# A hybrid encoder trunk: the first eight steps in a written order with x in eighths, and two pieces of background work put off by a step

## The chip, the cores and the metric

The kernel runs on one core of a Trainium2 chip. The metric is the device time in microseconds (us) of one execution, the median over runs. The engines are named as the profile names them: PE is TensorE (matmuls and transposes), PEld its weight loads, DVE is VectorE, ACT is ScalarE, POOL is GpSimd, SP is SyncE, which issues nearly all loads.

## The reference

Two layers over 256 tokens of width 2048, in float32. Each layer normalises x, projects it to queries, keys and values of three groups of heads, runs three kinds of attention (A: a window of 128 tokens with a sink and a learned bias; B: a neighbourhood on a grid with a learned bias; C: global, with normalised and rotated queries and keys), normalises each group's output, projects it back, and adds an MLP with a squared ReLU. Cut to what matters:

```python
for l in range(DEPTH):                      # DEPTH = 2
    h = rmsnorm(x, norm_mix[l])
    proj = h @ w_in[l]                      # 2048 -> 3840
    qa, ka, va, qb, kb, vb, qc, kc, vc = split(proj)
    oa = window_attention(qa, ka, va, a_sink[l], t5_table)        # 8 heads
    ob = neighborhood_attention(qb, kb, vb, b_rpb[l])             # 8 heads
    oc = axial_global_attention(qc, kc, vc, c_q_gain[l], c_k_gain[l])   # 16 heads
    mix = concat([rmsnorm(oa, out_gain_a[l]), rmsnorm(ob, out_gain_b[l]), rmsnorm(oc, out_gain_c[l])])
    x = x + mix @ w_o[l]
    h = rmsnorm(x, norm_mlp[l])
    u = relu(h @ w_up[l])                   # 2048 -> 8192
    x = x + (u * u) @ w_down[l]
return rmsnorm(x, norm_final)
```

## The kernel before

All of x (two tiles of 128 tokens) stays in the on-chip memory; the weights are streamed through once, in pieces of 512 KB. Every float32 product is made of three products of shorter numbers: a weight piece is split into a high part (ACT, line 823) and a low part (DVE, line 824), an activation likewise, and high x high, high x low and low x high are added up in PSUM.

One weight piece is one **step**. The list `steps` is walked in order (lines 852 to 871). Per layer, counted from 0: steps 0 to 59 are the input projection (queries of A, keys and values of A, keys and values of C, queries of C twice, values of B, and two chunks b0 and b1 with queries and keys of B); steps 60 to 67 the output projection of group A, 68 to 83 that of C, 84 to 91 that of B; then come the steps of the MLP. A step of the projections is 12 matmuls of 512 columns in `mode_b` (steps 8 to 11 have 24 of 256 columns), for each of the two token tiles in the order high-high, high-low, low-high per weight row block. A step's weights are loaded seven steps ahead and split two steps ahead.

Everything else (transposes, softmax, products with V, preparing a mixer block) is **background work**: `add` (line 150) puts a piece with a cost and a delay into the queue `bgq`, and `tick` (line 163), called after each step, moves a clock on by 2.6 and emits pieces that are due, from the front of the queue, until the next piece would exceed a budget of 2.2. `need(flag)` (line 176) is called before a step whose input must be there: while the flag is not set, it emits the piece at the front of the queue, whether due or not. A program-level scheduler then orders each engine's instructions near that order; on the chip each engine runs its own instructions strictly in order and waits on semaphores for the others.

One attention **unit** (four score blocks: four heads of one kind, or two heads for two query blocks in B) is three pieces: scores and softmax (`unit_scores`, lines 333 to 372: scores into the one score bank `S`, bias on DVE, row maximum, exponentials on ACT, reciprocal, normalising on POOL at line 372), transposes of the probabilities (`unit_transp`, line 381, split by ACT and DVE at 382 and 383), and the product with V (`unit_pv`, lines 393 and 400, summed by DVE at 408 and 413). Each layer has four units of B; they are called U1 to U4. After the last unit of a block of heads, `unit_pv` calls `u.finish`, which is `mix_prep` (line 417): it makes the high and low parts of the block (lines 423 and 424) and sums squares on POOL; with a group's last block it also sets the flag ("mix", layer, group), which the group's first output step needs.

The queries' transposes (`q_transposes`, lines 254 to 261) and the keys' (`k_transposes`, lines 269 to 276) of b0 and b1 are two pieces with the same delay after the projection's end. Transposes, products with V and the steps' results share six PSUM banks; a bank is free when DVE has read its last user.

The start: `hprep` transposes x, scales it by the norm's gain and splits it (lines 199 to 211), and sums squares of x (line 190) whose reciprocal root (line 244) is applied when a projection's result leaves PSUM (line 539). x is loaded in two pieces of 256 columns and three of 512, with weight pieces between them on SP's queue. A matmul with a bias table (line 136) is one more background piece.

## Time and profile before

| | us |
|---|---|
| median of 3 runs | 2062.93 (2062.06 to 2064.14) |
| the profiled execution | 2063.2 |
| its span in the profile | 2061.4 |
| PE busy | 2042.8 |
| DVE busy | 1337.5 |
| ACT busy | 1049.7 |
| POOL busy | 256.6 |

The span runs from the first to the last recorded instruction; 1.8 us of the execution's own time lie outside it. A busy time is the sum of an engine's instructions; PE's are pipelined, so two neighbours overlap in the record and the distance between their starts is what one costs. In rows of the timeline the first number is the start, the second the length, and the bracket at the end says how long the engine stood idle before and what ended that.

### The profile page before, as it was taken

How to read it: one execution, taken by the hardware profiler on the slowest of the kernel's cores; microseconds unless marked ns; L12 is line 12 of the kernel's file. 1: busy time of each engine (PE TensorE's matmuls, PEld its weight loads, DVE VectorE, ACT ScalarE, POOL GpSimd, SP SyncE). 2: the span in 40 equal slices, each digit the busy share in tenths (PEclk: the TensorE clock that was granted, in tenths of full speed). 3: DMA queues.
4: the chain of work that ended last, by engine and by line, in shares of the span. 5: the costliest groups of instructions: out<-in, count | busy, mean ns of one | idle time of the engine just before them, and what ended most of it. 6: DMA issues, size and time to landing. Idle time of an engine off the chain costs nothing.

```text
span 2061.4 us, 27426 instructions
## 1 busy us (share of the span) xinstructions
PE 2042.8 (99%) x10424; PEld 1739.4 (84%) x10424; DVE 1337.5 (65%) x1629; ACT 1049.7 (51%) x1544; POOL 256.6 (12%) x294
## 2 busy tenths in 40 slices
PE   8999999999999999999999999999999999999998
PEld 7888788888888888888888888888888888888887
DVE  6777976565565555656668789766565556556565
ACT  6667756444344444444556676555344444434444
POOL 0393330000000000000005744200000000000001
PEclk9999999999999999999999999999999999999999
DMA  8655465666666666666656463566666666666663
GB/s 285 179 169 157 155 192 179 190 186 192 195 186 194 192 194 192 187 194 186 188 178 183 152 181 113 184 184 185 195 188 194 189 194 192 186 195 186 193 212 123
DMA packets 107681, 381.26 MB, mean 185 GB/s; under 512 B 11891, under 2 KB 14707, under 8 KB 107548
## 3 DMA queue, kind: packets, MB, share of 16 engines
q1 hardware_dynamic: 107116, 378.41, 60.4%
q8 instruction: 82, 1.34, 0.3%
q10 hardware_dynamic: 432, 1.10, 0.1%
q14 instruction: 51, 0.42, 0.1%
HBM read 377.34 MB, written 2.11 MB: 184 GB/s over the span
## 4 chain that ended last, share of the span: by engine, by line
PE 96%; DVE 1%; ACT 1%; issue 1%; DMA 0%; SPq 0%; DVEq 0%; POOLq 0%; POOL 0%; ACTq 0%
PE mm L465 19%; PE mm L466 19%; PE mm L467 19%; PE mm L630 17%; PE mm L634 9%; PE S L630 6%; PE S L634 3%; PE tr L381 1%; PE tr L400 1%; PE S L339 1%; PE S L340 1%; PE tr L199 1%; DMA wraw<-in_w_in_dram 0%; DVE big L424 0%; PE tr L393 0%
## 5 line engine op out<-in xcount | busy, mean ns | idle before, releaser
L824 DVE TENSOR_TENSOR wlo<-wraw,whi 128x1024 fp32r<-128x1024 f32 (+1 forms) x697 | 861.0, 1237 | 648.5 <-ACT whi L823 640.4
L823 ACT CAST whi<-wraw 128x1024 fp32r<-128x1024 f32 (+1 forms) x697 | 730.5, 1050 | 913.9 <-PE mm L467 460.6
L465 PE MATMUL mm<-whi,big 128*128 128x512 f32 (+1 forms) x1800 | 696.7, 388 | 6.8 <-DVE big L261 3.7
L466 PE MATMUL mm<-wlo,big 128*128 128x512 f32 (+1 forms) x1800 | 694.8, 386 | 1.0 <-DVE wlo L824 0.9
L467 PE MATMUL mm<-whi,big 128*128 128x512 f32 (+1 forms) x1800 | 693.5, 385 | 0.0
L630 PE MATMUL mm<-big,whi 128*128 128x512 f32 x1536 | 417.0, 393 | 0.0
L465 PEld LDWEIGHTS mm<-whi,big 128*128 128x128 f32 x1800 | 338.9, 188 | 72.3 <-issue 4.1
L467 PEld LDWEIGHTS mm<-whi,big 128*128 128x128 f32 x1800 | 339.1, 188 | 67.7
L466 PEld LDWEIGHTS mm<-wlo,big 128*128 128x128 f32 x1800 | 339.4, 189 | 66.2 <-DVE wlo L824 2.1
L630 PEld LDWEIGHTS mm<-big,whi 128*128 128x128 f32 x1536 | 272.9, 189 | 44.5
L634 PE MATMUL mm<-big,wlo 128*128 128x256 f32 x1536 | 245.0, 282 | 0.0
L634 PEld LDWEIGHTS mm<-big,wlo 128*128 128x128 f32 x1536 | 227.7, 190 | 20.0
L630 PE MATMUL S<-big,whi 128*128 128x512 f32 x512 | 158.6, 390 | 0.0
L372 POOL TENSOR_SCALAR big<-big,sm 128x256 f32<-128x256 f32 x128 | 87.2, 699 | 244.3 <-DVE sm L370 156.0
L630 PEld LDWEIGHTS S<-big,whi 128*128 128x128 f32 x512 | 96.2, 188 | 22.0
L244 POOL TENSOR_TENSOR sm<-sm,mhalf 128x2 f32<-128x2 f32 (+2 forms) x12 | 12.3, 1029 | 780.9 <-DVE sm L239 767.4
L634 PE MATMUL S<-big,wlo 128*128 128x256 f32 x512 | 103.2, 283 | 0.0
L718 POOL TENSOR_TENSOR x<-x,big 128x512 f32<-128x512 f32 x6 | 8.6, 1454 | 718.1 <-ACT mid L725 718.1
L670 DVE SCALAR_TENSOR_TENSOR x<-mm,sm,x 128x512 f32<-128x512 f32 x127 | 89.2, 743 | 3.1 <-PE mm L467 3.1
L634 PEld LDWEIGHTS S<-big,wlo 128*128 128x128 f32 x512 | 79.4, 191 | 0.0
L361 ACT ACTIVATE big<-S,sm,rq 128x256 f32<-128x256 f32 x64 | 35.3, 561 | 19.9 <-DVE sm L347 17.2
L645 DVE SCALAR_TENSOR_TENSOR mid<-mid 128x512 f32<-128x512 f32 x64 | 43.9, 686 | 0.5
(127 smaller groups left out, 1185.6 us busy)
## 6 DMA issues: line engine op xcount, KB each, us to landing
wraw<-in_w_up_dram SPq DMA_DIRECT2D x256, 512.0 KB, 3.5
wraw<-in_w_down_dram SPq DMA_DIRECT2D x256, 512.0 KB, 3.5
wraw<-in_w_in_dram SPq DMA_DIRECT2D x119, 512.0 KB, 3.6
wraw<-in_w_o_dram SPq DMA_DIRECT2D x64, 512.0 KB, 4.3
biasB<-in_rpb_dram SPq DMA_DIRECT2D x16, 349.5 KB, 6.3
biasA<-avec SPq DMA_DIRECT2D x4, 768.0 KB, 4.8
x<-in_x_dram SPq DMA_DIRECT2D x3, 512.0 KB, 8.6
big<-in_gfin_dram SPq DMA_DIRECT2D x2, 512.0 KB, 5.6
```

Of the source, the lines that this page charges most:

```text
L199: last_tr[0] = nc.tensor.transpose(psv[:, kk, t, :], x[:, t, c0:c0 + P], ident).ins
L361: nc.scalar.activation(p[:, s, :], src[s], AF.Exp, bias=negm[:, s:s + 1], scale=u.rq[:, s:s + 1] if u.kind == "C" else 1.0, accum_out=sums ...
L372: nc.gpsimd.tensor_scalar(p[:, s, :], p[:, s, :], rs[:, s:s + 1], 1.0, op0=ALU.mult, op1=ALU.mult)
L465: nc.tensor.matmul(o, a_h, wh[:, i, :], start=first and i == 0, stop=False)
L466: nc.tensor.matmul(o, a_h, wl[:, i, :], start=False, stop=False)
L467: last_mm[0] = nc.tensor.matmul(o, a_l, wh[:, i, :], start=False, stop=last and i == len(sub) - 1).ins
L630: nc.tensor.matmul(box["b"][fs], wh[:, kk, fs * P:(fs + 1) * P], ht[:, kk, :], start=k == 0 and kk == 0, stop=False, skip_group_check=True)
L634: nc.tensor.matmul(box["b"][fs][:, 0:256], wl[:, kk, fs * P:(fs + 1) * P], ht[:, kk, 0:256], start=False, stop=k == 7 and kk == 1, skip_gr ...
L645: nc.vector.scalar_tensor_tensor(a, a, 0.0, a, op0=ALU.max, op1=ALU.mult)
L670: nc.vector.scalar_tensor_tensor(xs, box["b"][t], st["r2"][:, t:t + 1], xs, op0=ALU.mult, op1=ALU.add)
L823: last_hi[0] = nc.scalar.copy(h[:, part], w[:, part]).ins
L824: nc.vector.tensor_sub(lo[:, part], w[:, part], f(h[:, part]))
```

## The change

Three things are edited.

1. **The start.** x is loaded in eight parts of 256 columns, each ahead of a weight piece on SP's queue. The preparation of x for steps 0 to 7 is no longer in the background queue: `hprep(..., queue=False)` hands back two functions, and each of the first eight steps runs, between its high-high matmuls and the rest, a hook that issues the next block's transposes, the next step's split and one sum of squares. `pinned()` orders these on PE and ACT behind the last instruction of the written order, by edges without a semaphore. In these steps `mode_b` goes over both token tiles part by part: high-high, low-high, high-low.
2. **A finished block.** `u.finish(raw)` is no longer called at the end of `unit_pv`, but put into the background queue with cost 0 and delay 2.6.
3. **The keys' transposes** of b0 and b1 are due 2.6 after the queries' transposes were emitted, instead of together with them.

```diff
-    def hprep(key, gcol, j, hT, ss, done, fin_rs, late=0):
+    def hprep(key, gcol, j, hT, ss, done, fin_rs, queue=True):
...
+        if not queue:
+            return p, sq
+        a = add(lambda: p(0), 0.45, delay=D_X)
         add(p1, 0.45, after=(a,), delay=(0,))
...
         if u.last:
-            u.finish(raw)
+            add(lambda: u.finish(raw), 0.0, delay=2.6)
...
+        if hook[0]:
+            stop = "hl"
+            for part in ("hh", "lh", "hl"):
+                with pinned():
+                    ins = [one(t, i, part) for t in blocks for i in range(len(sub))]
+                last_pe[0] = ins[-1]
+                if part == "hh":
+                    hook[0]()
+            return
...
-                pk = add(lambda: k_transposes(qs, 2, 2, kh, kl), 0.45, delay=D_QK)
+                pk = add(lambda: k_transposes(qs, 2, 2, kh, kl), 0.45, after=(pq,), delay=(2.6,))
...
-    load_x(256, 512)
-    load(1)
-    nl = 2
-    for j in range(4):
-        if j:
-            load_x(j * 512, (j + 1) * 512)
-            load(nl)
-            nl += 1
-        hprep(0, 0, j, st0["hT"], st0["ss"], ("mix", 0), st0["rs_mix"], 6.0 + 4.0 * j)
-    emit(bgq[0])
+    for i in range(1, 8):
+        load_x(i * 256, (i + 1) * 256)
+        if i < 6:
+            load(i)
+    nl = 6
+    prep = [hprep(0, 0, j, st0["hT"], st0["ss"], ("mix", 0), st0["rs_mix"], queue=False) for j in range(4)]
+    prep[0][0](0)
...
+        if i < 8:
+            def between(i=i):
+                if i < 7:
+                    with pinned():
+                        prep[(i + 1) // 2][0]((i + 1) % 2)
+                with pinned():
+                    split(i + 1)
+                for j, t in ([((i - 1) // 2, (i - 1) % 2)] if i else []) + ([(3, 1)] if i == 7 else []):
+                    with pinned():
+                        prep[j][1](t)
+                    last_act[0] = last_sq[0]
+            hook[0] = between
+            ns = i + 2
```

How the program's instructions stand at three places follows. In these rows whi and wlo are the parts of a step's weights, mm and tr are banks with a step's results or with transposes and products with V, S is a unit's scores, and big, mid and sm are buffers of the activations. The lines of the changed kernel stand some lines lower: its 341 and 342 are the scores (339 and 340 before), 383 the transposes of the probabilities (381), 395 the products with V (393), and 465 all three kinds of matmul.

PE in layer 0 around step 68, the first output step of group C (whi_2572 before, whi_2566 in the changed kernel). Before, from the end of U3's scores, with U1's product with V (tr_2676) and U2's transposes (tr_2710):

```order
L340 MATMUL S_2606<-big_2267,big_2265 128x256
L465 MATMUL mm_2637<-whi_2572,big_1815 128x512
L466 MATMUL mm_2637<-wlo_2573,big_1815 128x512
...
L444 MATMUL tr_2651<-ones,sqacc_1822 128x64 x2
L465 MATMUL mm_2637<-whi_2633,big_2073 128x512
L465 MATMUL mm_2638<-whi_2633,big_2073 128x512
L393 MATMUL tr_2676<-big_2590,big_1596 128x256
...
L381 MATMUL tr_2710<-ident,big_2496 128x128 x4
```

The same place in the changed kernel, from the end of U3's scores (S_2600) over U1's product (tr_2627), U2's transposes (tr_2643), U4's scores (S_2700), U3's transposes and product (tr_2672, tr_2686) and U4's (tr_2727, tr_2741):

```order
L342 MATMUL S_2600<-big_2270,big_2268 128x256
L395 MATMUL tr_2627<-big_2584,big_1599 128x256
L383 MATMUL tr_2643<-ident,big_2499 128x128 x4
...
L341 MATMUL S_2700<-big_2269,big_2268 128x256
...
L383 MATMUL tr_2672<-ident,big_2609 128x128
...
L395 MATMUL tr_2686<-big_2670,big_1600 128x256
...
L383 MATMUL tr_2727<-ident,big_2709 128x128 x4
L383 MATMUL tr_2734<-ident,big_2709 128x128 x4
L395 MATMUL tr_2741<-big_2725,big_1600 128x256
L465 MATMUL mm_2767<-whi_2566,big_1876 128x512
```

What stood among steps 69 to 79 now stands ahead of the first matmul of step 68, in both layers.

DVE at the same place in the changed kernel, from U3's bias (S_2600) to U4's reduction:

```order
L353 SCALAR_TENSOR_TENSOR big_2609<-S_2600,big_2274 128x512 x2
L385 TENSOR_TENSOR big_2642<-tr_2643,big_2641 128x512
L360 TENSOR_REDUCE sm_2610<-big_2609 128x4
...
L372 RECIPROCAL sm_2619<-sm_2611 128x4
...
L385 TENSOR_TENSOR big_2671<-tr_2672,big_2670 128x512
L385 TENSOR_TENSOR big_2671<-tr_2679,big_2670 128x512
L353 SCALAR_TENSOR_TENSOR big_2709<-S_2700,big_2280 128x512 x2
L410 TENSOR_TENSOR mid_2697<-tr_2686,ot_2695 64x256 x2
L360 TENSOR_REDUCE sm_2710<-big_2709 128x4
```

U4's bias stands behind both subtractions of U3's transposes; before, low parts of step weights stood between these instructions.

DVE in layer 0 around step 62, before:

```order
L413 TENSOR_TENSOR mid_2183<-tr_2300,ot_2305 64x2x128 x2
L824 TENSOR_TENSOR wlo_2424<-wraw_2186,whi_2423 128x1024
L424 SCALAR_TENSOR_TENSOR big_2309<-mid_2183,gn,big_2309 128x256 x2
L261 TENSOR_TENSOR big_2265<-tr_2318,big_2265 64x2x256 x2
L604 SCALAR_TENSOR_TENSOR x<-mm_2286,sm_1420,x 128x512
L276 TENSOR_TENSOR big_2267<-tr_2327,big_2266 64x2x256 x4
L604 SCALAR_TENSOR_TENSOR x<-mm_2287,sm_1420,x 128x512
```

and in the changed kernel:

```order
L415 TENSOR_TENSOR mid_2186<-tr_2303,ot_2308 64x2x128 x2
L618 SCALAR_TENSOR_TENSOR x<-mm_2289,sm_1465,x 128x512
L837 TENSOR_TENSOR wlo_2427<-wraw_2189,whi_2426 128x1024
L263 TENSOR_TENSOR big_2268<-tr_2312,big_2268 64x2x256 x2
L618 SCALAR_TENSOR_TENSOR x<-mm_2290,sm_1465,x 128x512
...
L278 TENSOR_TENSOR big_2270<-tr_2402,big_2269 64x2x256 x4
L372 RECIPROCAL sm_2376<-sm_2368 128x4
L426 SCALAR_TENSOR_TENSOR big_2415<-mid_2186,gn,big_2415 128x256 x2
```

The finished block's rows (424, now 426) and the keys' subtractions (276, now 278) moved behind the queries' subtractions and the steps' evacuations.

ACT in layer 0 at the end of the written order, in the changed kernel, from the last block's split to the evacuation of the first projection:

```order
L218 ACTIVATE big_343<-tr_338,gn 128x256 x2
L836 CAST whi_348<-wraw_174 128x1024
L199 ACTIVATE mid_352,sm_89<-x,zero_85 128x512
L836 CAST whi_368<-wraw_204 128x1024
L199 ACTIVATE mid_372,sm_89<-x,zero_85 128x512
L199 ACTIVATE mid_374,sm_89<-x,zero_85 128x512
L836 CAST whi_419<-wraw_242 128x1024
L553 ACTIVATE big_390<-mm_146,sm_380 128x512
```

Before, the last squares (190) stood four casts ahead of the first evacuation (539); now one cast stands between them.

More of the change, by code (lines that the diff above doesn't have):

```diff
@@ L144, in tile_trunk, with pinned @@
     cur = [0.0]
-    last_hi, last_mm, last_tr, h_act = [None], [None], [None], []
+    last_sq, last_lo = [None], [None]
+    last_pe, last_act, hook = [None], [None], [None]
+    def pinned():
+        es = ExitStack()
+        if hook[0]:
+            for ins in (last_pe[0], last_act[0]):
+                if ins is not None:
+                    es.enter_context(tc.issue_after(ins))
+        return es
     class Piece:
@@ L182, in halves, with sq @@
         return rows.rearrange("p k (s c) -> p s k c", s=2)
-    def hprep(key, gcol, j, hT, ss, done, fin_rs, late=0):
-        def sq():
-            for t in range(NT):
-                junk = mid(F32, 512)
-                nc.scalar.activation(junk, x[:, t, j * 512:(j + 1) * 512], AF.Square, bias=zero1[:, 0:1],
-                                     accum_out=ss[:, t * 4 + j:t * 4 + j + 1])
+    def hprep(key, gcol, j, hT, ss, done, fin_rs, queue=True):
+        def sq(t):
+            junk = mid(F32, 512)
+            last_sq[0] = nc.scalar.activation(junk, x[:, t, j * 512:(j + 1) * 512], AF.Square, bias=zero1[:, 0:1],
+                                              accum_out=ss[:, t * 4 + j:t * 4 + j + 1]).ins
+            if (j, t) == (3, 1):
+                fin_rs()
         def half(h):
@@ L198, in half @@
                     c0 = (4 * j + 2 * h + kk) * P
-                    last_tr[0] = nc.tensor.transpose(psv[:, kk, t, :], x[:, t, c0:c0 + P], ident).ins
+                    tr = nc.tensor.transpose(psv[:, kk, t, :], x[:, t, c0:c0 + P], ident).ins
             rows = big(F32R, 2, 512)
@@ L206, in half @@
             for kk in range(2):
-                h_act.append(nc.scalar.activation(hh[:, 0, kk, :], src[kk], AF.Copy, scale=gs[kk]).ins)
+                act = nc.scalar.activation(hh[:, 0, kk, :], src[kk], AF.Copy, scale=gs[kk]).ins
+            last_pe[0], last_act[0] = tr, act
             for kk in range(2):
@@ L210, in half, with p @@
                                                op0=ALU.mult, op1=ALU.subtract)
-        def p0():
-            half(0)
-            flags.add((done, 2 * j))
+        def p(h):
+            half(h)
+            flags.add((done, 2 * j + h))
         def p1():
-            half(1)
-            if not late:
-                sums()
-            flags.add((done, 2 * j + 1))
-        def sums():
-            if late:
-                with tc.issue_after(last_hi[0]):
-                    sq()
-            else:
-                sq()
-            if j == 3:
-                fin_rs()
-        a = add(p0, 0.45, delay=D_X)
+            p(1)
+            sq(0)
+            sq(1)
+        if not queue:
+            return p, sq
+        a = add(lambda: p(0), 0.45, delay=D_X)
         add(p1, 0.45, after=(a,), delay=(0,))
-        if late:
-            add(sums, 0.0, delay=late)
     def mean_eps(ss, n_in, scale):
@@ L458, in mode_b, with one @@
     def mode_b(banks, h_tile, wh, wl, sub, first, last, n=512, blocks=(0, 1)):
-        for t in blocks:
-            o = banks[t][:, 0:n]
-            for i, kk in enumerate(sub):
-                a_h = h_tile[i][:, 0, kk, t * P:(t + 1) * P]
-                a_l = h_tile[i][:, 1, kk, t * P:(t + 1) * P]
-                nc.tensor.matmul(o, a_h, wh[:, i, :], start=first and i == 0, stop=False)
-                nc.tensor.matmul(o, a_h, wl[:, i, :], start=False, stop=False)
-                last_mm[0] = nc.tensor.matmul(o, a_l, wh[:, i, :], start=False, stop=last and i == len(sub) - 1).ins
+        def one(t, i, part):
+            kk = sub[i]
+            a = h_tile[i][:, int(part == "lh"), kk, t * P:(t + 1) * P]
+            return nc.tensor.matmul(banks[t][:, 0:n], a, (wl if part == "hl" else wh)[:, i, :],
+                                    start=first and i == 0 and part == "hh",
+                                    stop=last and i == len(sub) - 1 and part == stop).ins
+        if hook[0]:
+            stop = "hl"
[6 more added lines that the diff above has]
+            return
+        stop = "lh"
+        for t in blocks:
+            for i in range(len(sub)):
+                for part in ("hh", "hl", "lh"):
+                    one(t, i, part)
     state = {}
@@ L821, in split @@
         for part in ([slice(0, 1), slice(1, 2)] if i < 1 else [slice(0, s.kk)]):
-            with tc.issue_after(h_act[-1]) if i < 2 else nullcontext():
-                last_hi[0] = nc.scalar.copy(h[:, part], w[:, part]).ins
-            nc.vector.tensor_sub(lo[:, part], w[:, part], f(h[:, part]))
+            act = nc.scalar.copy(h[:, part], w[:, part]).ins
+            last_lo[0] = nc.vector.tensor_sub(lo[:, part], w[:, part], f(h[:, part])).ins
+        last_act[0] = act
         hi_t[i], lo_t[i] = h, lo
@@ L836, in tile_trunk @@
     load(0, halves=True)
-    load_x(256, 512)
-    load(1)
-    nl = 2
-    for j in range(4):
-        if j:
-            load_x(j * 512, (j + 1) * 512)
-            load(nl)
-            nl += 1
-        hprep(0, 0, j, st0["hT"], st0["ss"], ("mix", 0), st0["rs_mix"], 6.0 + 4.0 * j)
-    emit(bgq[0])
-    with tc.issue_after(last_tr[0]):
+    for i in range(1, 8):
[5 more added lines that the diff above has]
+    prep[0][0](0)
+    with tc.issue_after(last_pe[0]):
         for _ in range(N_WARM - 2):
-            nc.tensor.matmul(wb, warm[:, 0:P], warm, start=True, stop=True)
-    split(0)
+            last_pe[0] = nc.tensor.matmul(wb, warm[:, 0:P], warm, start=True, stop=True).ins
+    with tc.issue_after(last_act[0]):
+        split(0)
     ns = 1
@@ L857, in tile_trunk @@
             s.pre()
-        while ns < min(len(steps), i + LOOK_SPLIT) and i:
+        if i < 8:
[11 more added lines that the diff above has]
+            ns = i + 2
+        while ns < min(len(steps), i + LOOK_SPLIT):
             split(ns)
@@ L861, in tile_trunk @@
         s.mm(hi_t.pop(i), lo_t.pop(i))
-        if i == 0:
-            first_step = last_mm[0]
-            emit(bgq[0])
+        hook[0] = None
         if i == 2:
@@ L868, in tile_trunk @@
         if i == 8:
-            setup_tables()
-        with tc.issue_after(first_step) if i < 2 else nullcontext():
-            tick()
+            with tc.issue_after(last_lo[0]):
+                setup_tables()
+        tick()
 def _bucket_onehot():
```

## The prediction

> **What bounds the kernel now.** I read the page first: the span and the chain that ended last.

> ```profile
> span 2061.4 us, 27426 instructions
> PE 96%; DVE 1%; ACT 1%; issue 1%; DMA 0%; SPq 0%; DVEq 0%; POOLq 0%; POOL 0%; ACTq 0%
> ```

> The chain runs through TensorE (PE) for 96% of the span. The change removes no product (each step keeps its 12 matmuls), so it can only win where PE waits, and loses wherever it makes PE wait. Next I read who PE waits for, and the two places themselves in the timeline and in the table by stretch (PE, PEld, DVE, ACT, POOL busy, then granted clock, DMA share, GB/s).

> ```profile
> PE mm L465 <- DVE big L261: 3.7, 2, 1.9
> 1242.59 2.24 DVE L424 SCALAR_TENSOR_TENSOR big<-mid,gn,big 128x256 fp32r<-128x256 f32 x2
> 1244.84 1.39 DVE L261 TENSOR_TENSOR big<-tr,big 64x512 fp32r<-64x512 f32 x2
> 1246.38 0.47 PE L465 MATMUL mm<-whi,big 128*128 128x512 f32 x1 [1.87 <-DVE big L261]
> 225.00:230.00 5.00, 3.12 (x15) 2.54 (x14) 4.90 (x8) 3.47 (x6) 2.82 (x4) 1.00 0.91 334
> 1245.00:1250.00 5.00, 3.62 (x10) 2.95 (x11) 4.88 (x8) 2.86 (x5) 2.21 (x3) 0.72 0.11 43
> 1250.00:1255.00 5.00, 5.00 (x22) 4.04 (x21) 5.00 (x8) 2.26 (x3) 0.00 (x0) 0.94 0.02 3
> ```

> Once in each layer, at step 62, VectorE (DVE) prepares a finished mixer block (L424, 2.24 us) before it empties the bank of the queries' transposes (L261), and PE waits 1.9 us for that bank. In layer 1 the granted clock then falls to 0.72 and 0.94 of two 5 us stretches. At half speed that is 5 x 0.28 / 0.5 + 5 x 0.06 / 0.5 = 3.4 us slow, so 1.7 us lost. In layer 0 the same pause left the clock at 1.00. The other place is the start:

> ```profile
> 7.82 0.66 PE L199 MATMUL tr<-ident,x 128*128 128x128 f32 x4 [0.57 <-DMA x<-in_x_dram]
> 8.23 0.48 PE L466 MATMUL mm<-wlo,big 128*128 128x512 f32 x1
> 8.55 0.39 PE L467 MATMUL mm<-whi,big 128*128 128x512 f32 x1
> 8.78 0.39 PE L465 MATMUL mm<-whi,big 128*128 128x512 f32 x1
> 18.19 0.67 PE L465 MATMUL mm<-whi,big 128*128 128x512 f32 x1 [2.59 <-ACT big L207]
> 37.22 1.02 PE L136 MATMUL tr<-oh,t5x 33*8 33x512 f32 x2
> 38.17 1.09 PE L254 MATMUL tr<-ident,big 128*128 128x128 f32 x8
> ```

> A matmul costs 0.23 us (8.55 to 8.78), a step 12 x 0.23 = 2.74 us, four transposes 0.41 (7.82 to 8.23). PE idles 2.59 us before 18.19, and the transposes of the first queries, which follow step 7, start at 38.17.

> **The change part by part: the start.** The x loads and the written order of steps 0 to 7 go together. Each step now issues 4 matmuls, the next block's 4 transposes, 8 matmuls: 2.74 + 0.41 = 3.15 us. The ScalarE (ACT) side:

> ```profile
> 8.52 0.84 ACT L207 ACTIVATE big<-tr,gn 128x256 fp32r<-128x256 f32 x2 [1.53 <-PE tr L199]
> 9.24 1.05 ACT L823 CAST whi<-wraw 128x1024 fp32r<-128x1024 f32 x1
> 12.52 0.72 ACT L190 ACTIVATE mid<-x,zero 128x512 f32<-128x512 f32 x1
> 29.59 0.16 DVE L237 TENSOR_REDUCE sm<-sm 128x2 f32<-128x8 f32 x1 [0.18 <-ACT mid L190]
> 30.12 1.10 POOL L244 TENSOR_TENSOR sm<-sm,mhalf 128x2 f32<-128x2 f32 x1 [28.83 <-DVE sm L239]
> 36.03 0.69 ACT L539 ACTIVATE big<-mm,sm 128x512 f32<-128x512 f32 x1 [0.37 <-PE mm L467]
> ```

> From the transposes' start to the next high part it is 9.24 + 1.05 - 7.82 = 2.47 us, and the transposes start 0.92 into their step, so a step takes about 3.43, 0.28 more than PE's work. Step 0 starts at 6.5 as before (its loads stand in front of the queue as they did), step 1 at 10.3, step 6 at 27.5. The table's matmul (0.95, 37.22 to 38.17) now stands ahead of step 7, which ends near 27.5 + 3.15 + 0.95 + 2.74 = 34.3, about 3 us earlier than now. Then a new wait: the sums of squares of x are now spread over the steps, and the last ones come behind step 8's cast. ACT does, from about 30.9: one square, a cast, two squares, 3 x 0.72 + 1.05, to 34.1. The reduction to the reciprocal root took 30.12 + 1.10 - 29.59 = 1.6, the evacuation 0.69. So the queries' transposes start at 36.4: PE idles 2.1 us there, but is 1.8 ahead of 38.17. If the pause slows the clock, as 1.87 did in one case of two, 1.7 of it is given back. I take 1.0; ends 0.1 and 1.8. The loads stay ahead of this pace: a step needs 0.77 MB in 3.43 us, 230 GB/s, and 334 GB/s stands in a stretch above.

> [...]

> **Keys' transposes and the finished block put off.** At step 62 the L424 pair now comes later than L261, and the keys' subtractions a step later. DVE reaches L261's subtraction 2.24 us earlier, more than the 1.87 waited, so both pauses go: 1.88 + 1.87 + 1.7 for the clock = 5.4 us; 3.7 if the clock is not counted. The work itself stays, beside matmuls of steps 62 and 63.

> **What the put-off block does at step 68.** This is the term that decides. The block sets the flag ("mix", layer, "C") only when it runs. The last C unit's product with V is emitted after step 66; the block is then last in the queue. The tick after step 67 emits a set of transposes and one of scores, 2 x 0.87 = 1.74, and breaks off before the next piece of 0.87 because 2.61 exceeds 2.2. So step 68 finds no flag, and need() empties the queue from its front: everything left of the four B units, call them U1 to U4, stands in PE's order ahead of step 68: scores of U3 and U4, transposes of U2 to U4, products with V of all four. Before, these lay among steps 67 to 79. Now nothing but themselves hides their softmax. Durations, from the groups of 215 to 290 us and the timeline there:

> ```profile
> L351 DVE SCALAR_TENSOR_TENSOR big<-S,big 128x512 f32<-128x512 f32 x8 | 5.1, 679 | 0.0
> L358 DVE TENSOR_REDUCE sm<-big 128x4 f32<-128x1024 f32 x4 | 4.8, 1210 | 0.0
> L361 ACT ACTIVATE big<-big,sm 128x256 f32<-128x256 f32 x16 | 7.9, 499 | 1.1 <-DVE sm L358 1.1
> L382 ACT CAST big<-tr 128x512 fp32r<-128x512 f32 x12 | 6.5, 589 | 0.1
> L383 DVE TENSOR_TENSOR big<-tr,big 128x512 fp32r<-128x512 f32 x13 | 8.5, 682 | 0.2
> L403 ACT COPY ot<-tr 64x512 f32<-64x512 f32 x6 | 3.5, 583 | 1.5 <-PE tr L393 1.1 <-PE tr L400 0.3
> L408 DVE TENSOR_TENSOR mid<-tr,ot 64x256 f32<-64x256 f32 x6 | 2.5, 413 | 0.0
> L824 DVE TENSOR_TENSOR wlo<-wraw,whi 128x1024 fp32r<-128x1024 f32 x20 | 24.7, 1238 | 6.3 <-ACT whi L823 6.1
> L604 DVE SCALAR_TENSOR_TENSOR x<-mm,sm,x 128x512 f32<-128x512 f32 x14 | 10.1, 744 | 0.1
> 238.23 1.84 POOL L372 TENSOR_SCALAR big<-big,sm 128x256 f32<-128x256 f32 x4 [10.25 <-PE S L340]
> 245.50 2.97 POOL L372 TENSOR_SCALAR big<-big,sm 128x256 f32<-128x256 f32 x4 [5.44 <-PE tr L381]
> 258.13 3.91 POOL L372 TENSOR_SCALAR big<-big,sm 128x256 f32<-128x256 f32 x4 [6.84 <-DVE sm L446]
> 236.18 1.03 PE L381 MATMUL tr<-ident,big 128*128 128x128 f32 x8
> 236.97 0.36 PE L339 MATMUL S<-big,big 128*128 128x256 f32 x1
> 237.88 0.28 PE L340 MATMUL S<-big,big 128*128 128x256 f32 x1
> 252.64 1.12 PE L393 MATMUL tr<-big,big 128*128 128x256 f32 x8
> 253.60 0.71 PE L381 MATMUL tr<-ident,big 128*128 128x128 f32 x5
> ```

> On PE, eight transposes take 0.79, a unit's scores 1.0, its product with V 0.96. Let step 67 end at 0. U3's scores end at 1.0. U2 is no hindrance: its scores ended 238.0 and its rows were normalised at 248.5, 10.5 us later; two steps, a product, a set of transposes and step 67 are 9.9. DVE, in its order: an evacuation 0.74, U1's two subtractions 1.36, U3's bias 1.36, U2's first subtraction 0.68, U3's reduction 1.21, to 5.4. ACT's four exponentials 2.0, but DVE still does two sums, a subtraction and a low part (0.83 + 0.68 + 1.24) ahead of the reciprocal: 8.3. GpSimd (POOL) normalises in 1.84, 2.97 or 3.91; with DVE partly busy I take 2.97: 11.4. U3's transposes at half clock 1.6: 13.0. ACT's cast 0.59, DVE's two subtractions 1.36: 14.9. Only now DVE comes to U4's bias, though its scores are long done: 16.3. U3's sums 0.83, reduction 1.21, exponentials 2.0, reciprocal 0.2: 20.5. POOL, with DVE idle, 1.84: 22.4. U4's transposes at half clock 24.0, casts and the last subtraction, with a half of the C block between them, 1.7: 25.7. I take 25.5. PE's own work in it, which it owes anyhow: 2 x 1.0 + 3 x 0.79 + 3.5 x 0.96 + 4 x 0.23 of step 68 = 8.7. Lost: 16.8, and 1.7 for a clock that starts slow, 18.5 a layer, **37.0 us** in both.

> Bounds: with both normalisations at 1.84 and the clock full throughout, 1.1 + 1.7 + 2 x 0.8 less for transposes, so 14.1 a layer; with both at 3.91 and one more slow stretch, 0.9 + 2.1 + 1.7 more, 23.2.

> **The sum**, against the profiled execution's own 2063.2 us (span 2061.4 and 1.8 around it; the median of the runs shown is 2062.93): 2063.2 + 37.0 - 5.4 - 1.0 = 2093.8, so **2094 us**, 1.5% slower. With the bounds: 2063.2 + 28.2 - 5.4 - 1.8 = 2084 to 2063.2 + 46.4 - 3.7 - 0.1 = 2106.

> **The rivals.** (1) Faster: the forced pieces cost nothing, since PE is busy with them or the units' chains lie beside step 67. Then only the wins count: 2063.2 - 5.4 - 1.8 = 2056. It decides if the chain from U3's scores to U4's product fits in PE's 8.7 us; the rows above sum to three times that. (2) U3 and U4 overlap: if DVE took U4's bias right after U3's, U4's normalisation would follow U3's at 11.4 + 3.0 and its transposes end at 16, and 16 - 8.7 + 1.7 = 9 a layer would be lost: 2063.2 + 18 - 6.4 = 2075. Against it: in DVE's order U4's bias stands behind U3's two subtractions, which need U3's transposes. (3) Dearer: POOL takes 3.91 (the row at 258.13, beside a busy DVE) and the clock stays low for another stretch, 2106. For it: PE works in pieces under 1.1 us between pauses of up to 7. (4) The put-off doesn't do what it says, and PE still waits at step 62: 5.4 more, 2099, inside the range.

> **How the numbers follow.** Forecast with (4) 0.70, (3) 0.14, (2) 0.11, (1) 0.05. The range 2079 to 2107 holds the forecast's bounds and most of (3), and leaves (1) and (2) out. 0.2%, about 4 us, is what a measurement of this kernel can tell from no change; only (1) reaches there: faster 0.04, same 0.02, slower 0.94.

> **What would show it.** In the changed profile: no wait of L465 for the queries' subtraction; the first queries' transposes near 36.4 behind a pause of about 2 us; in both layers, near 245 and 1282, some 25 us in which PE is busy a third of the time at a low clock, with waits of transposes for POOL. PE 99% busy there would make the prediction wrong, as would a pause under 8 us in sum.

## The result and the profile after

| | before | after |
|---|---|---|
| median of the runs (us) | 2063.64 (2062.06 to 2064.14) | 2096.80 (2095.61 to 2097.91) |
| ratio, with its 95% interval | | 1.0162 (1.0149 to 1.0175) |
| the profiled execution | 2063.2 | 2096.18 |
| its span | 2061.4 | 2094.3 |

The change makes the kernel 1.6% slower, 33 us. The page of the changed kernel has TensorE (PE) on 93% of the chain of waits, where it was 96%:

```profile
span 2094.3 us, 27442 instructions
PE 93%; DVE 4%; ACT 2%; issue 1%; POOL 0%; DVEq 0%; POOLq 0%; ACTq 0%
```

The table of PE's waits (engine, line, what it waited for: us in total, times, longest) says for whom PE now stands idle. The wait of step 62 for the queries' subtraction (before: L261, 3.7 us) is no longer in it, and others have come, of which these are the largest:

```profile
PE tr L383 <- POOL big L374: 15.2, 4, 5.8
PE tr L395 <- DVE big L385: 4.0, 4, 1.7
PE tr L256 <- ACT big L503: 3.9, 2, 1.9
PE tr L383 <- DVE x L618: 1.7, 2, 0.9
PE tr L256 <- ACT big L553: 1.4, 1, 1.4
```

The waits for POOL are at step 68, where the queue is emptied. This is PE's timeline in layer 0, after step 67's last matmul at 246.79 (start, length, instruction, idle time before it and what ended that):

```profile
246.79 0.39 PE L465 MATMUL mm<-whi,big 128*128 128x512 f32 x1
...
249.91 1.57 PE L395 MATMUL tr<-big,big 128*128 128x256 f32 x8 [0.32 <-DVE big L385]
251.79 0.36 PE L341 MATMUL S<-big,big 128*128 128x256 f32 x1 [0.31 <-DVE big L353]
254.89 0.86 PE L395 MATMUL tr<-big,big 128*128 128x256 f32 x5 [1.66 <-DVE big L385]
257.56 2.05 PE L383 MATMUL tr<-ident,big 128*128 128x128 f32 x8 [1.81 <-POOL big L374]
260.07 2.76 PE L395 MATMUL tr<-big,big 128*128 128x256 f32 x8 [0.46 <-ACT big L384]
268.60 2.69 PE L383 MATMUL tr<-ident,big 128*128 128x128 f32 x8 [5.77 <-POOL big L374]
271.54 0.63 PE L465 MATMUL mm<-whi,big 128*128 128x512 f32 x1
...
274.14 0.40 PE L465 MATMUL mm<-wlo,big 128*128 128x512 f32 x1
```

The first L383 shown is U3's transposes, the second U4's; the L465 at 271.54 is the first matmul of step 68, and only from 274.14 is one issued every 0.23 us again. Layer 1 shows the same, with pauses of 1.82 and 5.77 before the same rows. GpSimd (POOL), DVE and the clock in that stretch, from the timeline and the table by stretch (PE, PEld, DVE, ACT, POOL busy, granted clock, DMA share, GB/s):

```profile
256.22 2.65 POOL L374 TENSOR_SCALAR big<-big,sm 128x256 f32<-128x256 f32 x4 [7.45 <-DVE sm L372]
268.06 1.84 POOL L374 TENSOR_SCALAR big<-big,sm 128x256 f32<-128x256 f32 x4 [9.20 <-DVE sm L372]
260.05 1.29 DVE L385 TENSOR_TENSOR big<-tr,big 128x512 fp32r<-128x512 f32 x2 [2.13 <-ACT big L384]
261.25 1.28 DVE L353 SCALAR_TENSOR_TENSOR big<-S,big 128x512 f32<-128x512 f32 x2
254.00:257.50 3.50, 0.86 (x5) 0.66 (x5) 3.47 (x6) 2.12 (x8) 1.28 (x2) 0.82 0.22 23
264.50:268.00 3.50, 0.00 (x0) 0.00 (x0) 1.25 (x2) 2.07 (x8) 0.00 (x0) 0.50 0.00 0
268.00:271.50 3.50, 2.90 (x9) 1.82 (x10) 0.36 (x1) 0.98 (x3) 3.44 (x6) 0.50 0.00 0
271.50:275.00 3.50, 3.50 (x16) 2.92 (x16) 3.50 (x7) 2.67 (x7) 3.20 (x4) 0.74 0.01 2
```

U4's bias (L353 at 261.25) stands on DVE behind U3's subtractions (L385 at 260.05), so U4's softmax cannot begin before U3's transposes are done: the two units run one after the other, and between 264.5 and 268 PE does nothing.

The two gains show as well. PE's rows of the first queries' transposes, of b1's in layer 0, which lie in step 61 and transpose the result of step 59, and of step 62's first matmul:

```profile
36.90 0.44 PE L256 MATMUL tr<-ident,big 128*128 128x128 f32 x2 [1.42 <-ACT big L553]
219.78 0.33 PE L256 MATMUL tr<-ident,big 128*128 128x128 f32 x1 [1.95 <-ACT big L503]
224.41 0.40 PE L465 MATMUL mm<-whi,big 128*128 128x512 f32 x1
```

The first queries' transposes stand 1.27 us earlier than before (38.17), and step 62 starts without a pause, 2.59 us earlier than before (227.00). But b1's queries' transposes start at 219.78 in both kernels: on the way the lead went into a pause of 1.95 us that the kernel before does not have, and its counterpart in layer 1 is 1.93.

### The profile page after: what moved, and what is told of

Same layout as the page of the kernel before. It is cut to its first block, busy times and chain, and to the rows that moved or that the text cites. A ratio compares the mean times of both kernels' runs of the same rounds, so it can differ in the third digit from the quotient of the medians.

```text
span 2094.3 us, 27442 instructions
## 1 busy us (share of the span) xinstructions
PE 2055.7 (98%) x10424; PEld 1743.1 (83%) x10424; DVE 1339.9 (64%) x1629; ACT 1047.5 (50%) x1544; POOL 243.8 (12%) x294
## 4 chain that ended last, share of the span: by engine, by line
PE 93%; DVE 4%; ACT 2%; issue 1%; POOL 0%; DVEq 0%; POOLq 0%; ACTq 0%
PE mm L465 54%; PE mm L644 17%; PE mm L648 9%; PE S L644 6%; PE S L648 3%; PE tr L383 1%; DVE wlo L837 1%; PE tr L402 1%; ACT big L363 1%; PE tr L210 1%; DVE big L385 1%; PE S L342 1%; PE S L341 1%; PE tr L395 0%; DVE sm L360 0%
## 5 line engine op out<-in xcount | busy, mean ns | idle before, releaser
L465 PE MATMUL mm<-whi,big 128*128 128x512 f32 (+1 forms) x3600 | 1109.5, 387 | 0.1
L465 PEld LDWEIGHTS mm<-whi,big 128*128 128x128 f32 x3600 | 670.6, 188 | 135.4 <-ACT whi L836 3.3
L465 PE MATMUL mm<-wlo,big 128*128 128x512 f32 (+1 forms) x1800 | 689.5, 385 | 0.0
L465 PEld LDWEIGHTS mm<-wlo,big 128*128 128x128 f32 x1800 | 338.8, 188 | 64.4 <-DVE wlo L837 0.3
L374 POOL TENSOR_SCALAR big<-big,sm 128x256 f32<-128x256 f32 x128 | 80.4, 645 | 264.7 <-DVE sm L372 241.6
L383 PE MATMUL tr<-ident,big 128*128 128x128 f32 x256 | 40.2, 295 | 17.8 <-POOL big L374 15.2
L383 PEld LDWEIGHTS tr<-ident,big 128*128 128x128 f32 x256 | 31.2, 148 | 26.6 <-POOL big L374 19.6
L385 DVE TENSOR_TENSOR big<-tr,big 128x512 fp32r<-128x512 f32 x64 | 41.6, 683 | 11.1 <-ACT big L384 10.8
```

What stands on the lines that cost most here:

```text
L374: nc.gpsimd.tensor_scalar(p[:, s, :], p[:, s, :], rs[:, s:s + 1], 1.0, op0=ALU.mult, op1=ALU.mult)
L383: nc.tensor.transpose(ps[:, c * P:(c + 1) * P], u.p[:, s, kb * P:(kb + 1) * P], ident)
L385: nc.vector.tensor_sub(u.pl[:, kb, :], ps, f(u.ph[:, kb, :]))
L465: return nc.tensor.matmul(banks[t][:, 0:n], a, (wl if part == "hl" else wh)[:, i, :], start=first and i == 0 and part == "hh", stop=last a ...
```

## The experiments

Theory: emptying the queue at step 68 costs the 36 to 38 us, the start and step 62 give a few back. Rivals: the put-off block costs something by itself; PE's low clock rather than the chain makes the stretch long; start or keys carry part of the loss. The kernel before was timed beside each: its median was 2063.21 in the first two groups and 2063.71 in the last (squares first, second trace).

### Only the wanted piece is emitted

```diff
     def need(flag):
         while flag not in flags:
-            emit(bgq[0])
+            emit(next((p for p in bgq if getattr(p, "sets", None) == flag), bgq[0]))
...
-            add(lambda: u.finish(raw), 0.0, delay=2.6)
+            add(lambda: u.finish(raw), 0.0, delay=2.6).sets = u.sets
```

`u.sets` is the flag of a group's last block, and None for the others.

> The changed kernel, but where step 68 finds the flag of the C block unset, only the piece that sets it is emitted, not the queue from its front. Start, keys and put-off block stay as in the change. Theory (the loss is the emptying of the queue): the 26.5 us from step 67's end to full flow shrink to the usual 2.7 us step, both layers lose nothing there, and the time is 2096.8 less 2 x 19 = 2058.8; with the start's 1.3 and step 62's two pauses kept it should come to 2056 to 2060. Rival (the put-off block itself, or a later mixer block, is what holds step 68: its low part and its sum of squares stand in front of the step): several us a layer stay, 2065 to 2075. Rival (the put-off is harmless and something else in the change costs): 2090 or more.

Measured: 2061.99 (2059.73 to 2063.15, 11 runs), ratio to before 0.9995 (0.9986 to 1.0004). The waits for POOL are gone from the table, and 2096.80 - 2061.99 = 34.8 us with them. The traces say much the same. From b1's queries' transposes to the first transposes of x for the MLP it is, in layer 0, 328.63 - 219.78 = 108.85 in the changed kernel and 310.34 - 219.46 = 90.88 here, 18.0 less; in layer 1 it is 18.1 less. So the emptied queue costs 17.4 (by the medians) to 18.0 us a layer. But the median lies above the 2056 to 2060 that I expected; only the profiled run, the lowest of 11, is inside. The next four experiments say why.

### The put-off block alone, and the change without it

```diff
-            u.finish(raw)
+            add(lambda: u.finish(raw), 0.0, delay=2.6)
```

This line alone was put into the kernel before:

> The kernel before with only the finished block put off; loads, start and keys as before. Theory: this part alone carries the loss, 2 x 19 = 38 us on 2063.6, less one or both pauses at step 62 (up to 5.4): 2096 to 2102. Rival (the loss needs the keys' later transposes too, which lengthen the queue by a step): below 2085. Rival (the loss comes from the start): 2063 or less.

Measured: 2098.89 (2097.84 to 2099.47, 4 runs), ratio 1.0173 (1.0159 to 1.0187). One line carries the whole loss. The wait at step 62 is not in its table, but ahead of b1's queries' transposes PE now waits 2.1 us in each layer. After two lines of the table follow step 62's first matmul and the subtraction of the queries:

```profile
PE tr L381 <- POOL big L372: 17.0, 6, 5.9
PE tr L254 <- ACT big L489: 4.2, 2, 2.1
226.83 0.40 PE L465 MATMUL mm<-whi,big 128*128 128x512 f32 x1
225.19 1.39 DVE L261 TENSOR_TENSOR big<-tr,big 64x512 fp32r<-64x512 f32 x2
```

Step 62 starts at 226.83, only 0.17 us earlier than before (227.00): the pause has not gone, it has moved to step 61. It does not need the written start: it is there without it. And the same line taken back, in the changed kernel:

```diff
-            add(lambda: u.finish(raw), 0.0, delay=2.6)
+            u.finish(raw)
```

> The changed kernel with the finished block prepared at once again; the written start and the later keys' transposes stay. Theory (the put-off block costs 19 us a layer, the rest gains): no emptied queue, so 2063.6 less the start's gain (1.3, given back at the wait of 1.9 before b1's queries if that wait is real) less what the keys alone save at step 62. If the pause at step 62 came from the block's pair ahead of the queries' subtraction, it comes back (1.9 a layer): 2061 to 2063. If it came from the keys, it stays away: 2057 to 2060. Rival (start or keys carry part of the 33 us lost): above 2066.

Measured: 2058.26 (2057.98 to 2058.64, 11 runs), ratio 0.9975 (0.9966 to 0.9984): start and keys gain 4.9 us together, faster than both kernels, and step 62 has no pause.

### The start alone and the keys alone

The start alone is the changed kernel with block and keys' transposes where they were; the keys alone is this line in the kernel before:

```diff
-                pk = add(lambda: k_transposes(qs, 2, 2, kh, kl), 0.45, delay=D_QK)
+                pk = add(lambda: k_transposes(qs, 2, 2, kh, kl), 0.45, after=(pq,), delay=(2.6,))
```

> The changed kernel with the finished block prepared at once and the keys' transposes where they were: the start alone. Theory (the start gains 1.27, as the two traces show at the first queries' transposes, and step 62 keeps its two pauses): 2063.2 less 1.3, 2061 to 2062.5, with a wait for the queries' subtraction of about 1.9 in each layer. Rival (the lead is given back ahead of step 62 also without the put-off block): 2063 or more. Rival (the later keys gain nothing and the start brings all of the 4.9 that start and keys gain together): 2058 to 2059.

> The kernel before with only the keys' transposes a step later. Theory (step 62's pauses of 1.88 and 1.87 come from the keys, not from the finished block's pair ahead of the subtraction, since start and keys together gained 4.9): 2063.2 less 3.7 to 5.4, 2058 to 2059.5, and no wait for the queries' subtraction in the trace. Rival (the pause needs the block's pair put off as well, as the prediction had it in one term): 2062 to 2063.5, with a wait of 1 to 1.9 left.

Measured: the start alone 2062.26 (2060.05 to 2063.91, 11 runs), ratio 0.9993 (0.9984 to 1.0002); the keys alone 2059.27 (2058.28 to 2060.34, 11 runs), ratio 0.9979 (0.9971 to 0.9988). The medians differ by 0.95 and 3.94 from before, 4.89 in sum beside the 4.95 of both together. The interval of the start alone reaches no change, but its trace agrees with 0.95: b1's queries start at 218.78, 1.0 ahead of before, and both pauses of step 62 are there:

```profile
PE mm L465 <- DVE big L263: 3.8, 2, 1.9
```

The keys alone take step 62's pause away, though the block's pair still stands ahead of the queries' subtraction on DVE:

```profile
224.29 0.40 PE L465 MATMUL mm<-whi,big 128*128 128x512 f32 x1
222.34 1.98 DVE L424 SCALAR_TENSOR_TENSOR big<-mid,gn,big 128x256 fp32r<-128x256 f32 x2
225.02 1.39 DVE L261 TENSOR_TENSOR big<-tr,big 64x512 fp32r<-64x512 f32 x2
```

The subtraction starts at 225.02, hardly earlier than before (225.46), yet step 62 starts at 224.29, ahead of it. So it was not DVE's lateness by itself. The banks in the programs say what it was: before, the first bank of step 62's results (mm_2407) is the one that the queries' transposes (tr_2318) had last; with the keys a step later the first bank (mm_2394 there) is the one that a product with V (tr_2300) had last, and DVE had read that by 221.65. With only the block put off it is still the queries' bank. So the later keys remove the pause, and the put-off block alone only moves it.

### Only the last block of a group put off

```diff
-            add(lambda: u.finish(raw), 0.0, delay=2.6).sets = u.sets
+            if u.sets:
+                add(lambda: u.finish(raw), 0.0, delay=2.6).sets = u.sets
+            else:
+                u.finish(raw)
```

> The kernel in which only the piece that sets the flag is emitted at step 68, and of the finished blocks only the last of each group is put off; the first C block is prepared at once. Theory (the wait of 1.97 of b1's queries' transposes for ACT comes from the first C block's pair on DVE, 1.32, which the put-off pushes in front of the last C unit's maxima): the wait is gone in both layers, and the time falls from 2062.0 to 2057.5 to 2059, in a narrow band of runs. Rival (the wait comes from the lead that the start gives, or from the later keys): the wait stays, 2061 to 2063.

Measured: 2058.84 (2058.37 to 2059.29, 10 runs), ratio 0.9976 (0.9966 to 0.9985). The wait ahead of b1's queries is gone and the runs lie within 0.9 us. What took its place, first in this kernel, then in the one that emits the wanted piece but puts every block off:

```profile
206.87 1.09 PE L402 MATMUL tr<-big,big 128*128 128x512 f32 x3 [1.07 <-DVE big L385]
200.11 2.14 DVE L429 SCALAR_TENSOR_TENSOR big<-mid,gn,big 128x256 fp32r<-128x256 f32 x2
```

```profile
219.46 0.33 PE L256 MATMUL tr<-ident,big 128*128 128x128 f32 x1 [1.97 <-ACT big L503]
208.71 1.32 DVE L426 SCALAR_TENSOR_TENSOR big<-mid,gn,big 128x256 fp32r<-128x256 f32 x2 [0.22 <-ACT big L425]
```

The first C block's pair takes DVE 2.14 us in the one place and 1.32 in the other. At 200.11 it delays one unit's product by 1.07 us; put off to 208.71 it stands in front of the last C unit's maxima and exponentials, which stand on ACT in front of the evacuation of b1's queries (L503), and PE waits 1.97 us at once. From the first queries' transposes to the MLP's first transposes in layer 1 the one takes 1329.06 - 37.54 = 1291.52, the other 1329.46 - 36.60 = 1292.86, 1.3 us more. The profiled executions differ by only 0.4 us (2059.29 and 2059.73), since the first queries came 0.9 later in the first, and the medians by 3.2. Where the rest comes from, a second trace of the latter kernel says.

### A second trace of one kernel

The kernel that emits only the wanted piece once more, with no edit:

> Once more the kernel in which only the piece that sets the flag is emitted, for a second trace of it. Its 11 runs lie between 2059.7 and 2063.2, while the kernels without a pause of about 1.9 us in step 59 or 62 lie within 1 us. Theory (after a pause of 1.9 to 2.0 the clock falls to half in some cases and stays full in others, 1.7 us each): a run near 2062 shows one of the two pauses followed by a window of low clock, a run near 2063.5 both, a run near 2060 none. Rival (the spread has another source): a run of 2062 with full clock in both windows.

Measured: 2062.04. PE's rows of b1's queries in layer 1, the stretch of 3.41 us in which most of the pause ahead of them lies, and the next one, first in the execution of 2059.73, then in that of 2062.04:

```profile
1238.59 0.33 PE L256 MATMUL tr<-ident,big 128*128 128x128 f32 x1 [1.96 <-ACT big L503]
1235.00:1238.41 3.41, 1.63 (x8) 1.01 (x6) 1.91 (x4) 2.75 (x9) 0.14 (x1) 1.00 0.60 185
1238.41:1241.82 3.41, 3.23 (x18) 2.62 (x19) 2.02 (x4) 3.35 (x7) 3.41 (x6) 1.00 0.30 119
```

```profile
1239.35 0.33 PE L256 MATMUL tr<-ident,big 128*128 128x128 f32 x1 [1.94 <-ACT big L503]
1236.32:1239.73 3.41, 1.47 (x7) 0.93 (x6) 1.38 (x3) 3.31 (x10) 0.71 (x2) 1.00 0.52 172
1239.73:1243.14 3.41, 3.41 (x11) 2.67 (x10) 2.07 (x4) 2.83 (x5) 3.41 (x6) 0.50 0.18 74
```

The same program and the same pause (1.96 and 1.94 us): once the clock stayed at 1.00, once it was at 0.50 for 3.41 us. The second cost 3.41 x 0.50 = 1.7 us, and between the first 8 and the last 10 us neither trace has another low stretch.

What differs is where the pause lies. Within one execution the clock changed only at moments that lie a whole number of 3.413 us apart: in the kernel before it fell at 18.36, 1247.16 and 2056.12, 360 and 237 times 3.413 from one another. In the second execution here the pause (1237.41 to 1239.35) lies whole between two such moments. In the first (1236.63 to 1238.59) the moment 1238.41, counted back from the fall at 2054.19, cuts it into 1.77 and 0.19. The same holds for all sixteen pauses of 1.87 to 2.08 us at step 61 or 62, two in each of eight traces: the four that lie whole between two moments were followed by 3.41 us at 0.50, the twelve that are cut, with at most 1.77 us on one side, by full clock. So in these traces a pause of 1.9 us was a draw between executions: free of this or 1.7 us dearer. The other 0.6 between the two executions lies ahead of this place (b1's queries of layer 1 stand 0.76 apart, those of layer 0 already 0.82). The draw fits the wide spread of the kernels with such a pause (3.4 us for this one, 3.9 for the start alone) beside 0.7 and 0.9 of two without. The keys alone, without it too, spread over 2.1; they keep the pause of 2.6 us in the first steps, but that this is the cause is not shown.

### The rows of B not normalised

```diff
-        for s in range(4):
+        for s in range(4 if u.kind != "B" else 0):
```

> The changed kernel, in which the B units' rows are not normalised (GpSimd's multiplication by the reciprocal sums is left out, 16 instructions of each layer; the output is that of unnormalised rows). Theory (the emptied queue is bound by the units' chain of scores, DVE, ACT, GpSimd, transposes): U3's 2.65 and U4's 1.84 leave the chain, 4.5 a layer, and up to 1 more for their hand-over; 2096.8 less 9 to 11 = 2086 to 2088. Rival (the stretch is bound by TensorE at half rate or by DVE, with GpSimd beside it): 2095 to 2097. Rival (TensorE gets its clock back when the pauses shrink from 5.8 and 1.8 to about 3.9 and nothing): 2 to 4 a layer more, down to 2080.

Measured: 2089.87 (2087.65 to 2090.84, 4 runs), ratio 1.0128 (1.0115 to 1.0142), 6.9 below the changed kernel by the medians and 8.5 by the profiled executions; the median lies above the 2086 to 2088 expected. From b1's queries to the MLP's first transposes layer 0 takes 104.52 (219.47 to 323.99), 4.3 less than 108.85; layer 1 takes 4.2 less. So POOL's 2.65 + 1.84 = 4.5 stand on the path, and the rival with TensorE or DVE as the bound (2095 to 2097) falls. How much of the 4.3 is POOL's alone stays open, since the low clock in that stretch also lasts only 10.2 us in place of 17.1; the 2 to 4 a layer more of the other rival did not come. PE still waits, now for the exponentials:

```profile
253.59 0.93 PE L383 MATMUL tr<-ident,big 128*128 128x128 f32 x4 [0.90 <-ACT big L363]
263.59 2.16 PE L383 MATMUL tr<-ident,big 128*128 128x128 f32 x8 [3.44 <-ACT big L363]
```

### PE kept busy in the pauses

```diff
             ps = tr_bank()
+            if kb == 0 and fill:
+                with tc.issue_after(last_pv[0]):
+                    for _ in range(fill.pop(0)):
+                        nc.tensor.matmul(ps, warm[:, 0:P], warm, start=True, stop=True)
```

`fill` is [0, 8, 22] while step 68's queue is emptied: so many matmuls of zeros ahead of the transposes of U2, U3 and U4.

> The changed kernel with 8 and 22 matmuls of zeros (0.23 each at full clock, read by nobody) in front of U3's and U4's transposes in the emptied queue: TensorE is kept busy in the two pauses for GpSimd (1.8 and 5.8). Theory (of the 19 us a layer, the low clock has its part: transposes of 2.05 and 2.69 in place of 0.8 to 1.1, and a slow first step 68): 2 to 4 a layer come back, 2096.8 less 4 to 8 = 2089 to 2093, and the granted clock stays over 0.9 in the stretch. Rival (the stretch depends on DVE, ACT and GpSimd alone, the clock is a by-product): 2095 to 2098. Rival (the clock stays low whatever runs, and the zeros take 0.46 each, 10 us for 22): 2100 to 2106.

Measured: 2095.72 (2094.68 to 2096.40, 4 runs), ratio 1.0155 (1.0141 to 1.0169). That is 1.1 below the changed kernel and inside the first rival's range (2095 to 2098), not in the 2089 to 2093 of the theory. PE's rows and the stretches of layer 0 follow, then two stretches of layer 1:

```profile
255.65 2.02 PE L389 MATMUL tr<-warm 128*128 128x512 f32 x8
257.62 2.13 PE L392 MATMUL tr<-ident,big 128*128 128x128 f32 x8
262.01 5.16 PE L389 MATMUL tr<-warm 128*128 128x512 f32 x22
267.94 1.80 PE L392 MATMUL tr<-ident,big 128*128 128x128 f32 x8 [0.77 <-POOL big L379]
264.50:268.00 3.50, 2.73 (x13) 1.94 (x12) 0.60 (x2) 2.08 (x8) 0.59 (x2) 1.00 0.00 0
268.00:271.50 3.50, 2.83 (x11) 1.78 (x12) 1.16 (x2) 1.78 (x5) 3.50 (x6) 0.81 0.01 2
271.50:275.00 3.50, 3.50 (x16) 2.95 (x16) 3.42 (x7) 1.88 (x5) 2.23 (x3) 0.71 0.02 5
1306.00:1309.50 3.50, 2.83 (x14) 1.76 (x15) 1.17 (x2) 1.78 (x5) 3.50 (x6) 1.00 0.01 2
1309.50:1313.00 3.50, 3.50 (x20) 3.00 (x19) 3.50 (x7) 2.50 (x6) 2.23 (x3) 1.00 0.02 5
```

The zeros (L389) run at 0.23 each and the granted clock stays at 1.00 up to 268, where it was 0.50 without them. But U3's transposes still take 2.13 us at full clock, since POOL hands over their rows until 256.28 + 2.65 = 258.93, and U4's lose only 0.9 of their 2.69. The total hides what the clock is worth, though. In layer 0 the clock still falls at the start of step 68 (0.81 and 0.71), after pauses of only 0.77 and 0.62. In layer 1, after the same pauses, it stays at 1.00, and from step 67's end to the MLP's first transposes that layer takes 79.79 us (1285.03 to 1364.82). Layer 0 takes 81.21 (247.04 to 328.25), and the layers of the changed kernel 81.61 (247.02 to 328.63) and 81.97 (1283.88 to 1365.85). So the layer whose clock stayed at 1.00 took 1.8 to 2.2 us less than the changed kernel's two, about the low end of the 2 to 4 that I expected. Layer 1 had lost as much just before: its pause of 1.94 ahead of b1's queries was followed by 0.50 from 1256.60 to 1260.01, which the changed kernel's profiled execution does not have.

### The squares ahead of the cast

The kernel with start and keys, and in step 7 this order on ACT:

```diff
-                with pinned():
-                    split(i + 1)
+                if i < 7:
+                    with pinned():
+                        split(i + 1)
                 for j, t in ([((i - 1) // 2, (i - 1) % 2)] if i else []) + ([(3, 1)] if i == 7 else []):
...
+                if i == 7:
+                    with pinned():
+                        split(i + 1)
```

> Start and later keys without the put-off block, and in step 7 the last two sums of squares stand ahead of step 8's cast on ACT, not behind it. Theory (the pause of 1.40 before the first queries' transposes hangs on ACT's cast and squares, then the reduction and POOL's power): a cast of 1.05 leaves that chain, the pause falls to about 0.4 and the time by 1.0, 2058.3 to about 2057.3. Rival (step 8 then waits for its weights, or the lead is given back before step 59): 2058 to 2059.

Measured: 2057.79 (2057.57 to 2057.90, 6 runs), ratio 0.9970 (0.9958 to 0.9982), the lowest of all kernels here.

```profile
36.24 0.44 PE L256 MATMUL tr<-ident,big 128*128 128x128 f32 x2 [0.71 <-ACT big L553]
```

Of the 1.40 us of the pause 0.7 are left, and 0.5 arrive at the end (2058.26 to 2057.79). So the last squares are on the path that the prediction named, at about half the price expected. The kernel before was 0.5 slower beside this kernel than beside the other, but the profiled executions agree that it gains (2058.53 and 2057.78).

## Why the prediction was right, point by point

The prediction was 2094 us (2079 to 2107); 2096.8 was measured. The kernels in between set its terms apart, as differences of medians:

| from | to | us | the prediction's term |
|---|---|---|---|
| before, 2063.21 | start alone, 2062.26 | -0.95 | -1.0 (ends -0.1 and -1.8) |
| start alone | start and keys, 2058.26 | -4.00 | -5.4 (or -3.7 without the clock) |
| start and keys | last blocks put off too, 2058.84 | +0.58 | none |
| last blocks put off | all blocks put off, 2061.99 | +3.15 | none |
| all put off, wanted piece only | the change, 2096.80 | +34.81 | +37.0 (28.2 to 46.4) |
| sum | | +33.59 | +30.6 |

The changed kernel was timed on its own beside a before of 2063.64, so its term can be off by some 0.4.

**The emptied queue** is the term that decided, and it came as worked out: the flag is unset at step 68, the B units stand one behind the other, U4's bias waits behind U3's subtractions. Against the trace, with step 67's end at 247.0 as 0: POOL is done with U3's rows at 11.9 (11.4 forecast), with U4's at 22.9 (22.4), and PE is in full flow at 27.1 (25.5, and 1.7 for the clock). POOL's pieces took 2.65 and 1.84 where I took 2.97 and 1.84. The size was 18.5 a layer; 17.4 was measured by medians, 18.0 in the traces. The part that I had put down to the clock, 1.7 and twice 0.8 for transposes at half rate, was too large: a layer in which the clock stayed full was 1.8 to 2.2 shorter. And that an idle DVE is why POOL takes 1.84 does not come out of the rows: at 268.06 in the changed kernel it took 1.84 with DVE idle, but at 238.23 before it took 1.84 beside a DVE that was busy all the time.

**The start** has the right sum from two terms that were off. The pause before the first queries was 1.42, not 2.1, and left the clock full. And their transposes start 1.27 ahead, where 1.8 was forecast: at 36.90, 0.5 later than 36.4. Steps follow one another in 3.50 us, where 3.43 was forecast, 0.07 each (the two numbers it was added up from, 2.47 and 0.92, give 3.39).

**Step 62** is where the prediction failed by a size and by its reason. Its sentence that DVE reaches the queries' subtraction 2.24 us earlier, and so both pauses go, is not what happens. With the keys alone DVE reaches it 0.4 earlier, and the pause is gone, since step 62 no longer needs that bank first; with the block alone DVE reaches it 0.3 earlier, and step 62 starts 0.17 earlier. The 4.0 measured lie near the 3.7 without the clock: the clock's 1.7 was counted as in the profiled execution, in full, while between executions it was a draw (0.50 for 3.41 us after four of the sixteen pauses).

**Missing** was what the put-off does to the first block of C: its pair on DVE now stands in front of the last C unit, and PE waits 1.9 us in step 61 of each layer (3.2 by the medians: 1.3 of it in the traces without a low stretch, and the rest is about what one low stretch costs, 1.7). I had followed the put-off block to step 62 and to step 68, but not the earlier blocks, which the same line moves.

That the sum came within 3 us of the measured difference is in part luck: the emptied queue cost 2.2 less than forecast, while the keys gained 1.4 less and the put-off blocks cost 3.7 that no term held.

The rivals: the pieces that cost nothing (2056) are out by the waits of 15.2 us; the overlap of U3 and U4 (2075) by L353 at 261.25; POOL at 3.91 (2106) by 2.65; that the pause of step 62 stays (2099) by its absence from the table of waits, where it was 3.7.

## What to carry to other kernels

A piece of background work that sets a flag must not be put at the end of a queue that is emptied from its front when the flag is wanted: either the queue hands out the wanted piece alone, or its delay is set against the step that wants it. When one line moves a kind of piece, follow every piece of that kind, not only the one for which it is moved. And look for what a wait needs, here one PSUM bank more, before the engine that is late is blamed. And when a wait is gone from the table, see whether PE also gets there earlier: the put-off block only moved the pause from step 62 to step 61.
